# A hybrid decoder layer in fp32 on one core: the memory norm moved behind the key matmuls, combinations of x on VectorE, and a memory region set apart for the first operands of three stages

## The chip, the cores and the metric

The kernel runs on one core of one Trainium2 chip (trn2). The metric is the device time of one execution in microseconds (us), lower is better. Engines are named as the profile names them: PE is TensorE (matmuls; PEld is its weight load), DVE is VectorE, ACT is ScalarE, POOL is GpSimd, SP is SyncE, which here only issues DMAs. Each engine runs its own instruction stream in order.

## What is computed

One decoder layer on x (1024 tokens by 1024 channels) with 256 memory tokens, cut to what matters here:

```
h = rms_norm(x, g_mix);  z = h @ w_in                       # 13,312 columns
ret  = swish(rg) * head_norm(retention(rq, rk, rv), g_ret)   # 4 heads, chunks of 128
da   = head_norm(diff_attention(dq, dk, dv, lam), g_diff)    # 4 heads, causal, ALiBi
kv   = rms_norm(mem, g_mem) @ w_mem_kv;  mk, mv = halves of kv
ca   = softmax(cq @ mk.T / 16) @ mv                          # 4 heads
x   += (g0*(ret @ w_ret_o) + g1*(da @ w_diff_o) + g2*(ca @ w_cross_o)) @ w_out
u    = relu(rms_norm(x, g_ffn) @ w_up);  x += (u*u) @ w_down  # 4096 wide
out  = rms_norm(x, g_final)
```

`rms_norm(m, g)` scales each token by r = 1/sqrt(mean(m*m) + 1e-6) and each channel by g. As r is one number for each token, it can be applied to the rows of a product as well as to its operand.

## The kernel before

All activations are held with channels on the partitions and tokens along the free dimension, in tiles of 128 x 512 (`t` is the half of the tokens). An fp32 operand is split into a high and a low part (`split`, lines 143 to 145: a CAST on ACT writes the high part, a subtraction on DVE the low part), and a product is three matmuls, high by high, high by low, low by high (`mm3`, lines 153 to 159). These three lines, L157 to L159, are where nearly all matmuls are recorded.

The two widest products, z (52 units of 256 columns) and the MLP's up projection (16 units), use a scheme of seven block products in place of eight (`seven`, line 243). For each unit `left_operands` (line 210) loads two blocks of weights (tile `wr`), forms their combinations (`ws`) and splits seven operands into tiles `wo`, of which 11 exist; `quad` multiplies one of them with one of seven combinations of the input (`hop`). These combinations (B11, B21, T1 to T4, B22) are made once, ahead of the stage.

The stages follow each other in this order, with the lines of their code:

- **Start** (lines 283 to 413). `mt`, the memory tokens, are summed in squares (`wide_sums`), `rms_finish` makes the row factors, and `scale_rows` makes the normed tokens `mh`. Then come 8 key blocks (`mem_keys`) and 4 heads of values (`mem_values`); their results leave PSUM through `kv_store` (L377, a copy on ACT into one of three `kvs` tiles) and go to DRAM (`mk_d`, `mv_d`). Between them the generator `x_steps` norms x and makes the combinations of x; two of them for each `kp` are subtractions on POOL (L361, L362).
- **z** (lines 416 to 484). Results go to DRAM (`zh_d` holds q of the cross attention already split).
- **Cross attention** (from line 573). `cross_inputs` loads and splits mk and mv of a head, `cross_probs` loads q (`cq`) and computes the scores `csc`, and `cross_values` transposes the probabilities (`ctp`).
- **Differential attention**, with matmuls of the cross branch's output projection as filler.
- **Retention** (lines 809 to 965), 32 steps of a chunk each. `rec_load` (L828) loads a chunk's record (1280 KB) on ACT's DMA queue into one of three `rec` tiles, `ret_prepare` computes the scores `rsc`, `ret_product` the states `rst`. The filler is the rest of the branch projections (`y`).
- **Output projection and second norm** (lines 969 to 1024). Row sums of squares are added on POOL (`acc`, L1006); the new residual goes to DRAM (`xs_d`).
- **Up** (lines 1027 to 1048). The last two combinations of the normed x (`df`, L1044) are subtractions on POOL; `u_emit` stores u to DRAM.
- **Down** (lines 1051 to 1117). `down_chunk` loads u (into `ur`) and w_down (into `dwr`) and splits them into `u` and `dw`; chunks hold 2, 2, 4, 4, ... blocks of 128 rows of w_down (`CHUNKS`). The accumulators `x2` (tiles `xm`) are loaded with the residual first (L1106, 16 DMAs of 256 KB), and each chunk's product is added to them (L162, `xm<-xm,dn`). The final norm works on two halves of the last columns.

Pools on the "right" side are opened and closed stage by stage, so a tile of the next stage can be filled only when the memory of the stage before it has been released. A scheduler fixes the order of the instructions on each engine and DMA queue when the kernel is built; the DMAs of SP's queue are issued in that order, and one that waits holds back those behind it.

## Time and profile before

| | us |
|---|---|
| median of 3 runs | 2685.02 |
| lowest and highest | 2679.22, 2689.7 |
| the profiled execution, its own time | 2690.2 |
| its span in the profile | 2688.2 |
| PE busy in it | 2565.5 |
| mean granted clock of PE | 0.983 |

The span runs from the first to the last instruction. A row of the timeline gives the start of a piece of work, its length, and in square brackets how long its engine stood idle ahead of it and what ended that wait. "Busy" of PE is the time in which at least one matmul was under way, at either clock; matmuls overlap, so the mean duration of one is longer than the distance between two. The profiled execution took 5.2 us more than the median.

### The profile page before, as it was taken

What the parts mean: (1) busy time and instruction counts of PE and PEld (TensorE: products, weight loads), DVE (VectorE), ACT (ScalarE), POOL (GpSimd) and SP (SyncE); (2) the same over time, 40 slices, a digit from 0 to 9 for tenths busy, and PEclk for the clock granted to TensorE, in tenths of its full rate; (3) what the DMA queues carried; (4) which work ended last, traced back from release to release, by engine and by line L of the source; (5) the groups of instructions that cost most, each with busy time, mean ns of one, the idle gap of its engine ahead of it and who ended that gap; (6) DMA issues with size and microseconds to landing.
All of it is one profiled execution on the core that took longest, in us unless ns stands there. A gap on an engine that the chain in (4) does not pass through costs nothing. (4 is left out here: it accounts for less than half of the span.)

```text
span 2688.2 us, 32542 instructions
## 1 busy us (share of the span) xinstructions
PE 2565.5 (95%) x11878; PEld 2100.5 (78%) x11878; DVE 1588.2 (59%) x2831; ACT 1055.4 (39%) x1942; POOL 119.4 (4%) x125
## 2 busy tenths in 40 slices
PE   7899999999999999899996999999979999899998
PEld 6688887788888888688885787878868888688887
DVE  6666656665566544276774666663676565654435
ACT  4444444444344444355553223231544444311212
POOL 3000000000000000000110000000230000000001
PEclk9999999999999999999998999999989999999999
DMA  5444457755543333264448776753523332632311
GB/s 208 155 167 162 166 154 204 212 163 154 145 118 114 109 111 100 100 263 165 171 157 308 252 239 240 255 175 95 176 98 115 112 107 79 240 114 85 110 40 63
DMA packets 250416, 416.63 MB, mean 155 GB/s; under 512 B 16912, under 2 KB 147984, under 8 KB 242064
## 3 DMA queue, kind: packets, MB, share of 16 engines
q1 hardware_dynamic: 231680, 351.60, 40.3%
q10 hardware_dynamic: 18576, 62.96, 6.6%
q8 instruction: 93, 1.52, 0.2%
q14 instruction: 67, 0.55, 0.1%
HBM read 273.98 MB, written 140.51 MB: 154 GB/s over the span
## 5 line engine op out<-in xcount | busy, mean ns | idle before, releaser
L157 PE MATMUL x<-hop,wo 128*128 128x512 f32 x1904 | 751.7, 395 | 15.6 <-ACT wo L144 13.9
L158 PE MATMUL x<-hop,wo 128*128 128x512 f32 x1904 | 751.2, 395 | 0.0
L159 PE MATMUL x<-hop,wo 128*128 128x512 f32 x1904 | 745.2, 391 | 0.3 <-DVE wo L145 0.3
L157 PEld LDWEIGHTS x<-hop,wo 128*128 128x128 f32 x1904 | 359.1, 189 | 93.8 <-ACT wo L144 14.3
L159 PEld LDWEIGHTS x<-hop,wo 128*128 128x128 f32 x1904 | 358.6, 188 | 81.7 <-DVE wo L145 2.1
L158 PEld LDWEIGHTS x<-hop,wo 128*128 128x128 f32 x1904 | 359.1, 189 | 74.3
L144 ACT CAST wo<-wr 128x512 fp32r<-128x512 f32 x272 | 168.1, 621 | 242.0 <-PE x L159 233.6
L145 DVE TENSOR_TENSOR wo<-ws,wo 128x512 fp32r<-128x512 f32 x204 | 140.8, 692 | 197.4 <-ACT wo L144 197.3
L145 DVE TENSOR_TENSOR wo<-wr,wo 128x512 fp32r<-128x512 f32 x272 | 186.3, 687 | 92.1 <-ACT wo L144 92.0
L157 PE MATMUL dn<-u,dw 128*128 128x512 f32 (+1 forms) x544 | 206.7, 380 | 10.0 <-DVE xm L162 5.3
L158 PE MATMUL dn<-u,dw 128*128 128x512 f32 (+1 forms) x544 | 206.3, 379 | 0.0
L159 PE MATMUL dn<-u,dw 128*128 128x512 f32 (+1 forms) x544 | 206.0, 379 | 0.0
L162 DVE TENSOR_TENSOR zo<-x,s 128x512 f32<-128x512 f32 x156 | 107.6, 690 | 157.3 <-ACT s L272 109.7
L162 DVE TENSOR_TENSOR xm<-xm,dn 128x512 f32<-128x512 f32 (+1 forms) x152 | 99.0, 657 | 145.0 <-PE dn L159 138.7
L144 ACT CAST wo<-ws 128x512 fp32r<-128x512 f32 x204 | 126.3, 621 | 91.0 <-PE x L159 85.2
L157 PEld LDWEIGHTS dn<-u,dw 128*128 128x128 f32 x544 | 103.1, 189 | 31.0 <-DVE xm L162 6.8
L162 DVE TENSOR_TENSOR g<-y,g 128x512 f32<-128x512 f32 x64 | 44.2, 690 | 129.9 <-PE y L159 96.0
L159 PEld LDWEIGHTS dn<-u,dw 128*128 128x128 f32 x544 | 103.0, 189 | 19.9 <-DVE dw L145 0.8
L158 PEld LDWEIGHTS dn<-u,dw 128*128 128x128 f32 x544 | 103.1, 189 | 19.1 <-issue 0.2
L157 PE MATMUL y<-ar,whl 128*128 128x512 f32 x256 | 102.2, 400 | 9.1 <-ACT ar L144 9.1
L158 PE MATMUL y<-ar,whl 128*128 128x512 f32 x256 | 101.4, 396 | 1.4 <-DVE ar L145 1.4
L159 PE MATMUL y<-ar,whl 128*128 128x512 f32 x256 | 100.6, 393 | 0.0
(235 smaller groups left out, 4057.6 us busy)
## 6 DMA issues: line engine op xcount, KB each, us to landing
wr<-in_w_z SPq DMA_DIRECT2D x104, 512.0 KB, 4.0
rec<-rc ACTq DMA_DIRECT2D x32, 1280.0 KB, 7.8
zh<-zh SPq DMA_DIRECT2D x48, 512.0 KB, 3.4
rc<-zth SPq DMA_DIRECT2D x96, 256.0 KB, 3.6
rc<-zh SPq DMA_DIRECT2D x64, 256.0 KB, 3.7
g<-z SPq DMA_DIRECT2D x64, 256.0 KB, 4.1
wr<-in_w_up SPq DMA_DIRECT2D x32, 512.0 KB, 4.0
u<-uo ACTq DMA_DIRECT2D x64, 256.0 KB, 2.0
```

Source lines behind the costliest of these rows:

```text
L144: nc.scalar.copy(out=hl_hi, in_=src)
L145: eng.tensor_tensor(out=hl_lo, in0=src, in1=hl_hi.bitcast(F32), op=ALU.subtract)
L157: nc.tensor.matmul(out, ah, bh, start=first, stop=False, skip_group_check=again)
L158: nc.tensor.matmul(out, ah, bl, start=False, stop=False, skip_group_check=again)
L159: nc.tensor.matmul(out, al, bh, start=False, stop=last, skip_group_check=again)
L162: nc.vector.tensor_tensor(out=out, in0=a, in1=b, op=op)
```

## The change

It has six parts.

1. The memory tokens are only multiplied by `g_mem` ahead of the key and value matmuls. Their norm (`mem_norm`) is computed after the matmuls of the first key block, and is applied in `kv_store`: to keys by a DVE multiplication with a row (`mem_row`), to values by the scale of the ACT copy (`mem_r`).
2. The two POOL subtractions of each step of x, and the eight POOL subtractions `df` ahead of up, become DVE subtractions (`add`).
3. A pool `c0` of one tile (`ahead`) stays open from the end of the start stage to the end of the output projection. Before the z stage ends it takes the first q of the cross attention and the split keys of head 0; after the cross attention it takes the record of the first retention chunk. To make room, `wo` has 9 tiles in place of 11.
4. A pool `d0` holds the first block of w_down and of u, loaded and split while up runs; the first two chunks of down hold 1 and 3 blocks in place of 2 and 2.
5. u is loaded straight into the low half of its tile and split there, without the `ur` staging tile.
6. The first chunk's product is copied from PSUM into `x2` by ACT; the residual is loaded later (`xres`) and added by POOL after chunks 3 and 4.

```
-    *_, acc = wide_sums(mt)
-    add(acc[:, :NMEM], acc[:, :NMEM], acc[:, NMEM:HALF])
-    rb = rms_finish(acc, NMEM)
...
-        scale_rows(mem_of(k), src, vec[:, V_MEM + k : V_MEM + k + 1], rb[:, :NMEM])
+        nc.vector.tensor_scalar(
+            out=mem_of(k), in0=src, scalar1=vec[:, V_MEM + k : V_MEM + k + 1], scalar2=None, op0=ALU.mult
+        )
...
-            nc.gpsimd.tensor_tensor(out=b12, in0=b22, in1=b12, op=ALU.subtract)
-            nc.gpsimd.tensor_tensor(out=t4, in0=b21, in1=t2, op=ALU.subtract)
+            add(b12, b22, b12, ALU.subtract)
+            add(t4, b21, t2, ALU.subtract)
...
+    def mem_norm():
+        *_, acc = wide_sums(mt)
+        add(acc[:, :NMEM], acc[:, :NMEM], acc[:, NMEM:HALF])
+        nc.scalar.copy(out=mem_row, in_=rms_finish(acc, NMEM, mem_r)[:, :NMEM])
+
+    def kv_store(dst, o, r):
         st = sp0.tile([P, 256], F32, tag="kvs", name="kvs", bufs=3)
-        nc.scalar.copy(out=st, in_=o)
+        if r is None:
+            add(st, o, mem_row, ALU.mult)
+        else:
+            nc.scalar.activation(out=st, in_=o, func=AF.Copy, scale=r)
         nc.sync.dma_start(out=dst, in_=st)
...
+    c0p = cx.enter_context(tc.tile_pool(name="c0p", bufs=1, side="right", reuse_waits="tile"))
...
+    def z_between(i):
+        if i == NU - 3:
+            c = ahead_tile()
...
+            nc.sync.dma_start(out=q.bitcast(F32), in_=zh_d[CQ][0])
+            raw = zt.tile([P, HALF], F32, tag="zo", name="mkr", bufs=4)
+            nc.sync.dma_start(out=raw, in_=mk_d[0].rearrange("p d c -> p (d c)"))
...
-        q = load(qk_tile("q", "cq"), zh_d[CQ + h * 256][t])
+        q = ahead["q"] if h == t == 0 else load(qk_tile("q", "cq"), zh_d[CQ + h * 256][t])
...
+            if h == NH - 1 and i == 4:
+                ahead["rec"] = ahead_tile()
+                nc.sync.dma_start(out=ahead["rec"][:, :C_G].bitcast(F32), in_=rc_d[0][0][:, 0, :C_G])
...
-    for c in range(3):
+    recs.append(ahead["rec"])
+    for c in range(1, 4):
         rec_load(0, c)
...
-            if n + 2 < 8 * NH:
+            if 1 < n < 8 * NH - 2:
                 rec_load((n + 2) // 8, (n + 2) % 8)
...
+    CHUNKS = [range(0, 1), range(1, 4)] + [range(f, f + FC) for f in range(4, 32, FC)]
...
+                u = pool.tile([P, 2, HALF], F32R, tag="u", name="u", bufs=2 if c == 0 else 4 * FC)
+                nc.sync.dma_start(out=u[:, 1].bitcast(F32), in_=u_d[f][t])
+                split(u[:, 0], u[:, 1], u[:, 1].bitcast(F32))
...
+    def u_between(i):
+        if i == 13:
+            ahead["down"] = down_chunk(0, d0)
...
-            nc.gpsimd.tensor_tensor(out=df, in0=x3[kp][t][:, 1], in1=x3[kp][t][:, 0], op=ALU.subtract)
+            add(df, x3[kp][t][:, 1], x3[kp][t][:, 0], ALU.subtract)
...
-            add(x2[d][t][:, cols], x2[d][t][:, cols], o[:, :width])
+            if first:
+                nc.scalar.copy(out=x2[d][t], in_=o)
+            else:
+                add(x2[d][t][:, cols], x2[d][t][:, cols], o[:, :width])
...
+            if c in (3, 4):
+                for d in range(8):
+                    xr = zs_tile("sp", "xres", 3)
+                    nc.sync.dma_start(out=xr, in_=xs_d[d][c - 3])
+                    nc.gpsimd.tensor_tensor(out=x2[d][c - 3], in0=x2[d][c - 3], in1=xr, op=ALU.add)
```

`z_between` and `u_between` are called by `seven` after each unit; in `left_operands`, `bufs=11` becomes `bufs=9`.

How the change moves instructions is shown at three places. The first is SP's queue at the end of z, before the change: the last stores of z, a weight of the cross branch (`wst`), the keys and values of head 0 (`raw`) and the two halves of its q (`cq`).

```order
L427 DMA z_1_132<-zo 128x512 [waits DMAHW5_49,Activation_49]
L520 DMA g<-z_0_125 128x512 [waits DMAHW7_49,Pool_49]
L499 DMA wst<-in_w_co 128x1024 [waits DMAHW6_49]
L568 DMA raw<-mk_253 128x512 [waits DMAHW7_49]
L568 DMA raw<-mv_257 128x512 [waits DMAHW0_49]
L563 DMA cq<-zh_0_77 128x2048 [waits DMAHW1_49,PE_49]
L563 DMA cq<-zh_1_78 128x2048 [waits DMAHW2_49]
```

The same place of SP's queue after the change.

```order
L451 DMA z_1_132<-zo 128x512 [waits DMAHW6_49,Activation_49]
L556 DMA g<-z_0_125 128x512 [waits DMAHW7_49,Pool_49]
L535 DMA wst<-in_w_co 128x1024 [waits DMAHW0_49]
L604 DMA raw<-mv_257 128x512 [waits DMAHW1_49]
L599 DMA cq<-zh_1_78 128x2048 [waits DMAHW2_49]
L604 DMA raw<-mk_254 128x512 [waits DMAHW3_49]
```

The keys of head 0 and the first half of q stand earlier in the queue now, and the second half of q comes behind one load fewer of 256 KB and one fewer of 1 MB. On PE, 6 of the 24 first score matmuls now stand inside the last z unit and 18 right behind it.

The second place is PE at the change from differential attention to retention, before: `dot` are the last transposes of the attention, `y` the filler.

```order
L774 MATMUL dot<-ident,don 128x128 [waits Activation_49]
L774 MATMUL dot<-ident,don 128x128
L157 MATMUL rsc<-rec 128x128 [waits DMAHW5_49]
L158 MATMUL rsc<-rec 128x128
L159 MATMUL rsc<-rec 128x128
L157 MATMUL rsc<-rec 128x128
L158 MATMUL rsc<-rec 128x128
L159 MATMUL rsc<-rec 128x128
L157 MATMUL y<-ac_0_8861,whl 128x512 [waits DVE_49]
```

And after the change.

```order
L159 MATMUL y<-ac_1_8887,whl 128x512
L157 MATMUL rsc<-rec 128x128 [waits DMAHW6_49]
L158 MATMUL rsc<-rec 128x128
L159 MATMUL rsc<-rec 128x128
L157 MATMUL rsc<-rec 128x128
L158 MATMUL rsc<-rec 128x128
L159 MATMUL rsc<-rec 128x128
L157 MATMUL rst<-ahead 128x512
L158 MATMUL rst<-ahead 128x512
L159 MATMUL rst<-ahead 128x512
L157 MATMUL rst<-ahead 128x512 [waits DVE_49]
```

The scores of the first chunk (`rsc<-ahead`, 6 matmuls) have moved up among the attention's last matmuls. At the old place now stand the scores of the second chunk, which wait for that chunk's record, and six state matmuls of the first chunk ahead of `y`.

The third place is SP's queue where up ends and down begins, before.

```order
L1062 DMA ur<-u_0_173 128x512 [waits DMAHW1_49,DMAHW0_49,PE_49]
L1062 DMA ur<-u_1_174 128x512 [waits DMAHW5_49,DMAHW1_49]
L1067 DMA dwr<-in_w_down 128x1024 [waits DMAHW3_49,DVE_49,Pool_49]
L1062 DMA ur<-u_0_175 128x512 [waits DMAHW4_49]
L1062 DMA ur<-u_1_176 128x512 [waits DMAHW5_49]
L1067 DMA dwr<-in_w_down 128x1024 [waits DVE_49,DMAHW6_49,Activation_49,Pool_49]
L1106 DMA xm_0_19342<-xs_0_237 128x512 [waits DMAHW7_49]
L1106 DMA xm_1_19343<-xs_1_238 128x512 [waits DMAHW0_49,PE_49,Pool_49]
```

And after the change.

```order
L214 DMA wr<-in_w_up 128x1024 [waits DMAHW4_49]
L1162 DMA xres<-xs_0_237 128x512 [waits DMAHW5_49,DMAHW3_49,DMAHW6_49,DMAHW1_49,DMAHW7_49,DMAHW0_49,Activation_49]
L1080 DMA dwr<-in_w_down 128x1024 [waits DMAHW4_49,PE_49]
L1083 DMA u<-u_0_175 128x512 [waits DMAHW5_49]
L1083 DMA u<-u_1_176 128x512 [waits DMAHW7_49,DVE_49,Pool_49]
L1080 DMA dwr<-in_w_down 128x1024 [waits DMAHW0_49]
```

The first block's loads (`u_0_173`, `u_1_174` and its `dwr`) have moved up among the weight loads of up, the 16 `xm` loads are gone from here, and one `xres` load stands ahead of the second block's.

## Rows read from the trace of the kernel before

**Rows 1.** Page part 1: busy time of the engines over the span.

```profile
PE 2565.5 (95%) x11878; PEld 2100.5 (78%) x11878; DVE 1588.2 (59%) x2831; ACT 1055.4 (39%) x1942; POOL 119.4 (4%) x125
```

**Rows 2.** Timeline of PE, start stage (start, length, engine, line, work, idle before).

```profile
14.07 11.68 PE L384 MATMUL mk<-mh,kst 128*128 128x256 f32 x46 [0.57 <-DVE mh L200]
...
44.43 1.05 PE L170 MATMUL ssq<-ones,sqw 128*128 128x1 f32 x8 [1.50 <-DVE sqw L162]
...
93.26 0.79 PE L157 MATMUL x<-hop,wo 128*128 128x512 f32 x1 [6.34 <-ACT wo L144]
```

**Rows 3.** Timeline of PE, z to cross attention.

```profile
1143.32 0.55 PE L157 MATMUL csc<-mk,cq 128*128 128x256 f32 x1 [11.25 <-DMA cq<-zh]
...
1153.14 0.47 PE L157 MATMUL csc<-mk,cq 128*128 128x256 f32 x2 [0.81 <-DMA cq<-zh]
```

**Rows 4.** Timeline of PE, into retention.

```profile
1432.16 0.47 PE L157 MATMUL rsc<-rec 128*128 128x128 f32 x1 [6.28 <-DMA rec<-rc]
...
1436.97 0.79 PE L157 MATMUL y<-ac,whl 128*128 128x512 f32 x1 [3.27 <-DVE g L162]
```

**Rows 5.** Timelines of PE and POOL, start of up.

```profile
1981.81 0.79 PE L157 MATMUL x<-hop,wo 128*128 128x512 f32 x1 [7.53 <-ACT wo L144]
...
1994.52 2.05 PE L183 MATMUL rb<-dg,ones 128*128 128x512 f32 x2 [3.37 <-DVE dg L179]
...
1986.78 5.70 POOL L1044 TENSOR_TENSOR df<-x 128x512 f32<-128x512 f32 x3 [2.29 <-DVE hop L145]
```

**Rows 6.** Group of PE, 2306 to 2350 us, start of down (busy, mean ns; idle, releasers).

```profile
L157 PE MATMUL dn<-u,dw 128*128 128x512 f32 x44 | 18.7, 428 | 9.6 <-DVE xm L162 5.0 <-ACT dw L144 4.7
```

**Rows 7.** Groups of the start stage: PE, ACT, POOL (columns as before).

```profile
L394 PE MATMUL mv<-kst,mh 128*128 128x256 f32 x128 | 28.9, 383 | 7.1 <-ACT kvs L377 7.1
...
L144 ACT CAST hop<-xr 128x512 fp32r<-128x512 f32 x16 | 9.6, 618 | 9.9 <-POOL xr L203 4.8 <-POOL xr L361 3.6 <-DVE xr L200 1.5
L144 ACT CAST hop<-tt 128x512 fp32r<-128x512 f32 x12 | 7.3, 618 | 9.4 <-POOL tt L362 6.5 <-DVE hop L145 1.8 <-DVE tt L162 1.1
...
L361 POOL TENSOR_TENSOR xr<-xr 128x512 f32<-128x512 f32 x4 | 6.5, 1630 | 6.2 <-DVE tt L162 6.2
L362 POOL TENSOR_TENSOR tt<-xr,tt 128x512 f32<-128x512 f32 x4 | 6.5, 1630 | 3.3 <-DVE tt L162 1.9 <-ACT hop L144 1.4
```

**Rows 8.** Timeline of DVE, start stage.

```profile
57.19 0.68 DVE L145 TENSOR_TENSOR hop<-tt,hop 128x512 fp32r<-128x512 f32 x1
57.79 1.78 DVE L145 TENSOR_TENSOR hop<-xr,hop 128x512 fp32r<-128x512 f32 x1
```

**Rows 9.** DMA issues of 1135.9 and 1136.3 us (KB, us to landing).

```profile
cq<-zh SPq DMA_DIRECT2D x1, 1024.0 KB, 7.3
...
cq<-zh SPq DMA_DIRECT2D x1, 1024.0 KB, 9.4
```

**Rows 10.** Windows of PE: length, busy (matmuls), granted clock, DMA share, GB/s.

```profile
1143.30:1146.30 3.00, 2.98 (x14) 0.50 0.98 363
...
2311.00:2314.30 3.30, 3.24 (x7) 0.50 0.67 250
2314.50:2317.80 3.30, 3.30 (x16) 1.00 0.76 255
```

**Rows 11.** DMA issue of 1425.9 us: the second record.

```profile
rec<-rc ACTq DMA_DIRECT2D x1, 1280.0 KB, 10.2
```

**Rows 12.** Timeline of SP's queue, start of down.

```profile
2307.60 12.98 SPq L1106 DMA_DIRECT2D xm<-xs  x16
```

**Rows 13.** Groups of ACT by shape, whole span.

```profile
L144 ACT CAST wo<-wr 128x512 fp32r<-128x512 f32 x272 | 168.1, 621 | 242.0 <-PE x L159 233.6 <-DMA wr<-in_w_z 5.2 <-issue 3.1
...
L272 ACT COPY s<-x 128x512 f32<-128x512 f32 x68 | 39.9, 586 | 152.2 <-PE x L159 152.2
...
L144 ACT CAST dw<-dwr 128x1024 fp32r<-128x1024 f32 x32 | 33.0, 1051 | 165.9 <-PE dn L159 136.9 <-DMA dwr<-in_w_down 28.1 <-DVE xm L162 0.9
```

**Rows 14.** Window in down: length, then busy of PE, PEld, DVE, ACT, POOL; clock, DMA.

```profile
2420.00:2500.00 80.00, 80.00 (x355) 66.24 (x354) 36.56 (x52) 16.32 (x23) 0.00 (x0) 1.00 0.26 82
```

More of the change, by code (lines that the diff above doesn't have):

```diff
@@ L162, in add, with rms_finish @@
         nc.vector.tensor_tensor(out=out, in0=a, in1=b, op=op)
-    def rms_finish(acc, width):
+    def rms_finish(acc, width, keep=None):
         nt = width // P
@@ L174, in rms_finish @@
         )
-        r = tiny_tile(4, "rr")
+        r = tiny_tile(4, "rr") if keep is None else keep
         nc.gpsimd.tensor_tensor(out=r[:, :nt], in0=v[:, :nt], in1=mhalf[:, :nt], op=ALU.pow)
@@ L223, in left_operands @@
         ):
-            w = pool.tile([P, 2, HALF], F32R, tag="wo", name="wo", bufs=11)
+            w = pool.tile([P, 2, HALF], F32R, tag="wo", name="wo", bufs=9)
             split(w[:, 0], w[:, 1], src)
@@ L241, in quad, with seven @@
             )
-    def seven(units, ops, load, tmp, emit):
+    def seven(units, ops, load, tmp, emit, between=None):
         def begin(u):
@@ L413, in hybrid_block, with ahead_tile @@
     start.close()
+    cx = ExitStack()
+    c0p = cx.enter_context(tc.tile_pool(name="c0p", bufs=1, side="right", reuse_waits="tile"))
+    ahead = {}
+    def ahead_tile():
+        return c0p.tile([P, C_N], F32R, tag="c0", name="ahead")
     zw = ExitStack()
@@ L573, in cross_inputs @@
     def cross_inputs(h):
-        mk = load_halves(cp.tile([P, 2, 2, NMEM], F32R, tag="k", name="mk", bufs=2), mk_d[h])
+        mk = ahead["mk"] if h == 0 else load_halves(cp.tile([P, 2, 2, NMEM], F32R, tag="k", name="mk", bufs=2), mk_d[h])
         mv = load_halves(cp.tile([P, 2, 2, 256], F32R, tag="mv", name="mv", bufs=2), mv_d[h])
@@ L1024, in hybrid_block @@
     wpx.close()
+    cx.close()
+    d0 = ctx.enter_context(tc.tile_pool(name="d0", bufs=1, side="right", reuse_waits="tile"))
     ux = ExitStack()
@@ L1029, in hybrid_block, with down_chunk @@
     ut = ux.enter_context(tc.tile_pool(name="ut", bufs=2, side="right", reuse_waits="tile"))
+    FC = 4
+    CHUNKS = [range(0, 1), range(1, 4)] + [range(f, f + FC) for f in range(4, 32, FC)]
+    def down_chunk(c, pool):
+        ws, us = [], [[], []]
+        for f in CHUNKS[c]:
+            raw = pool.tile([P, 1024], F32, tag="wr", name="dwr", bufs=1 if c == 0 else 2)
+            nc.sync.dma_start(out=raw, in_=w_down[f])
+            for t in range(2):
+                u = pool.tile([P, 2, HALF], F32R, tag="u", name="u", bufs=2 if c == 0 else 4 * FC)
+                nc.sync.dma_start(out=u[:, 1].bitcast(F32), in_=u_d[f][t])
+                split(u[:, 0], u[:, 1], u[:, 1].bitcast(F32))
+                us[t].append(u)
+            w = pool.tile([P, 2, 1024], F32R, tag="w", name="dw", bufs=1 if c == 0 else FC + 2)
+            split(w[:, 0], w[:, 1], raw)
+            ws.append(w)
+        return ws, us
+    def u_between(i):
+        if i == 13:
+            ahead["down"] = down_chunk(0, d0)
     def u_emit(u, n, t, a, b):
@@ L1055, in hybrid_block, with mlp_down @@
     x2 = [[dw.tile([P, HALF], F32, name=f"xm{d}_{t}", tag=f"xm{d}_{t}", bufs=1) for t in range(2)] for d in range(8)]
-    def down_chunk(c):
-        ws, us = [], [[], []]
-        for f in CHUNKS[c]:
-            for t in range(2):
-                raw = dw.tile([P, HALF], F32, tag="ur", name="ur", bufs=4)
-                nc.sync.dma_start(out=raw, in_=u_d[f][t])
-                u = dw.tile([P, 2, HALF], F32R, tag="u", name="u", bufs=4 * FC)
-                split(u[:, 0], u[:, 1], raw)
-                us[t].append(u)
-            raw = dw.tile([P, 1024], F32, tag="wr", name="dwr", bufs=2)
-            nc.sync.dma_start(out=raw, in_=w_down[f])
-            w = dw.tile([P, 2, 1024], F32R, tag="w", name="dw", bufs=FC + 3)
-            split(w[:, 0], w[:, 1], raw)
-            ws.append(w)
-        return ws, us
-    def mlp_down(chunk, t, c0=0, width=HALF):
+    def mlp_down(chunk, t, c0=0, width=HALF, first=False):
         ws, us = chunk
@@ L1101, in final_norm @@
             nc.sync.dma_start(out=outT[k0 : k0 + n, :, c : c + width].rearrange("k p c -> p k c"), in_=y)
-    nxt = down_chunk(0)
-    for d in range(8):
-        for t in range(2):
-            nc.sync.dma_start(out=x2[d][t], in_=xs_d[d][t])
+    nxt = ahead["down"]
     for c in range(len(CHUNKS)):
@@ L1109, in hybrid_block @@
         if c + 1 < len(CHUNKS):
-            nxt = down_chunk(c + 1)
+            nxt = down_chunk(c + 1, dw)
             for t in range(2):
-                mlp_down(cur, t)
+                mlp_down(cur, t, first=c == 0)
+            if c in (3, 4):
[3 more added lines that the diff above has]
+                    nc.gpsimd.tensor_tensor(out=x2[d][c - 3], in0=x2[d][c - 3], in1=xr, op=ALU.add)
     mlp_down(cur, 0)
```

22 lines of the change are left out of this document (15 added, 7 removed).

## Prediction

> **What bounds the kernel now.** First the busy times of the page: PE works for 2565.5 of 2688.2 us, DVE for 59%, ACT for 39%, POOL for 4% [rows 1]. No part of the change takes a matmul away, so PE's busy time stays, and what can be won is PE's idle time (2688.2 - 2565.5 = 122.7 us) and what it costs that the granted clock is low after some of it. So the next view is the timeline of PE, read for rows with a long wait in brackets. The change aims at five of these places: the start (6.34 us ahead of the first z matmul [rows 2], and 7.1 us among the value matmuls [rows 7]), z to cross attention, 11.25 us [rows 3], into retention, 6.28 and 3.27 us [rows 4], the start of up, 7.53 and 3.37 us [rows 5], and the start of down, 9.6 us in all [rows 6]. They sum to 54.5 us; for each the reader should see what ends the wait: a DMA, ACT, or DVE. Last come the windows, which tell the clock: 14 matmuls in 3.0 us at a granted clock of 0.50, that is 1.2 of 2.4 GHz, and in down 7 matmuls in 3.3 us at 0.50 against 16 at 1.00 [rows 10].
>
> **Start.** The key matmuls begin at 14.07 after waiting for DVE [rows 2], and no longer need the norm of the memory, so the first block can begin some us earlier, when its weights are there. I give this lead no value: PE's next wait is for the squares of x from DVE, as at 44.43 [rows 2], and DVE's chain up to there is not shortened. It gets up to eight key multiplications, each at most the 0.68 us of a subtraction twice as wide [rows 8]; not all lie ahead of that point, and I charge 0.7 us. The gain is behind it. The value matmuls stand idle for 7.1 us, waiting for the copies `kvs` on ACT [rows 7]; in ACT's queue these stand behind casts that waited 3.6 and 6.5 us for the POOL subtractions L361 and L362 [rows 7]. These POOL operations take 1.63 us each [rows 7], and a DVE subtraction takes 1.78 us in place of 0.68 while POOL works [rows 8]. With eight of them moved, DVE saves 8 x 1.1 = 8.8 us and pays 8 x 0.68 = 5.4. So DVE gains 3.4 us and ACT's 10.1 us of waits shrink; I take 4.7 of PE's 7.1 us, less 0.7: **4 us**. Bounds: 0, if casts still arrive late from a DVE that has more to do, and 7.1. The 6.34 us ahead of z stay, because the first weights are issued behind the last `kvs` store in both.
>
> What DVE pays beside POOL can be weighed against a rule. The row shows a loss of 1.1 us for one DVE operation beside a POOL operation of 1.63 us [rows 7, 8]. The Trainium skill (SBUF — State Buffer, "Who interferes with whom") says that a DVE instruction with two SBUF inputs and a GpSimd one that reads SBUF lock each other out, the later one waiting for the whole of the earlier. By that rule a DVE operation could lose up to 1.63 us, the moved ones would free 8 x 1.63 - 5.4 = 7.6 us of DVE in place of 3.4, and the start would give about 7 us. I keep the row.
>
> **z to cross attention.** z ends at 1143.32 - 11.25 = 1132.07, and PE waits for the first half of q [rows 3], which lands at 1135.9 + 7.3 = 1143.2; the second lands at 1136.3 + 9.4 = 1145.7 [rows 9]. With the first half and the keys of head 0 loaded during z, 24 matmuls run at once and PE waits for the second half. This now stands where the first stood, with 256 KB fewer ahead (0.7 us at 363 GB/s [rows 10]): about 1142.5. Before, the second group began after 24 matmuls, 16 of them at half clock: 1143.3 + 4.9 = 1148.2. That is 5.7 us, to which come 8 transposes already done (0.9), while the second group now meets the half clock (-1.6): **5 us**. Bounds: 0, if the queue holds the second half as late as it held both; 8, if also the 0.81 us at 1153.14 [rows 3] goes and the transposes' wait for the softmax is free. The six score matmuls inside the last z unit cost nothing: they are moved, not added. The nine `wo` tiles are a rival below.
>
> **Into retention.** The first record is loaded during the attention, but the matmuls at the old place now need the second record. That is issued first on ACT's queue, so it lands where the first did, 1432.1, instead of 1425.9 + 10.2 = 1436.1 [rows 4, 11]. So the 6.28 us stay (and the six moved matmuls leave it a little longer). Six state matmuls now run ahead of `y`, and every load behind has 1280 KB less ahead of it, some 3.5 us; they can fill most of the 3.27 us [rows 4] and more later, and I take **2.5 us**. Bounds: +6 if the later records' lead carries on, -3 if the load during the attention delays its own loads.
>
> **Start of up.** Three POOL subtractions hold POOL for 5.70 us, and the second norm's factor is queued behind them; its wait on PE is 3.37 us [rows 5]. Both go, but the eight subtractions (8 x 0.68 = 5.4 us) stand in DVE's queue ahead of the low part of the second `wo`, for which PE waits after its first matmuls. What is gained at the second norm is waited for there: **0.5 us**, bounds -1.5 and 3.
>
> **Start of down.** Here 9.6 us are idle, 4.7 for ACT's cast of the first weights and 5.0 for DVE, which waits for the residual [rows 6], 16 loads that hold SP's queue for 12.98 us [rows 12]. Two stretches of 3.3 us at half clock lose about half of each, 3.4 us in all (one shown [rows 10]). So 13 us could go. In their place comes a new wait: ACT must copy 16 results of the first chunk (0.586 us each, 9.4 us), and cast three weights (3 x 1.05) and six u (6 x 0.62) [rows 13], 16.2 us in order, while the first chunk's 48 matmuls take 11. Some 5 us of it ends late, and one stretch of half clock may stay (1): **7 us**. Bounds: 3, where the second block's weights come late too, as one `xres` load that waits for the last u stores stands ahead of them; 12. The 16 POOL additions later cost PE nothing: at up to 1.1 us of DVE each they take 18 us in two chunks of some 44 us, and DVE is busy for 36.56 of 80 us there [rows 14].
>
> **The sum.** 4 + 5 + 2.5 + 0.5 + 7 = 19 us. The profiled execution took 2690.2 us, so 2671.2 on its terms; it lies 5.2 above the median of 2685.0, so **2666 us** for the median.
>
> **Rivals.** *The gains are taken back by what is late next* (same). ACT bounds the first two chunks of down, which then give 3, and in the start DVE's longer chain leaves 0; with 5 + 2.5 + 0.5 that is 11 us: 2674. For it: ACT's 16.2 us against 11. Against it: PE has the second chunk, 33 us long, in which ACT can catch up. Chance 0.2. *It does not do what it says at the two record places* (same): PE waits as long for the second half of q and the second record as it did for the first, so that only 4 + 0.5 + 7 = 11.5 us come: 2673.5. For it: the 6.28 us that I leave in place; against it: the order of the queues. Chance 0.13. *Nine tiles are too few* (slower). `wo` serves 68 units in z and up. ACT's casts into it already wait 233.6 us for PE to release a tile [rows 13], so the number of tiles does bind ACT. A tile less means that each cast comes one quad of 12 matmuls later, about 2.85 us ((1132.07 - 93.26) / 52 units / 7 quads). With nine, a released tile is needed again eight quads on, 22 us, against 0.62 + 0.69 us for the split; only if other work delays ACT by over 20 us would PE wait. If each unit waited 0.5 us, it would be 34 us: 2666 + 34 = 2700. Chance 0.04.
>
> **The numbers.** Forecast 0.6; rivals 0.2, 0.13 and 0.04; 0.03 is for what I have not seen. A change of 0.5%, 13.4 us, is about what a measurement of this kernel can tell. Faster by that means under 2671.6: **0.6**. Within it: 0.2 + 0.13 + 0.02 = **0.35**. Slower: 0.04 + 0.01 = **0.05**. All upper bounds together would give 36 us (2649), all lower ones -1.5 (2687); as neither end is likely for five places at once, I take **2652 to 2682**, which takes in the two rivals on the same side and leaves out the slower one.
>
> **What would show it.** In the new profile: the value matmuls with under 3 us of waits; the second score group starting near 1142.5 less what the start gave; a wait of about 6 us still ahead of the second record; the first `dn` matmul right behind the last of up, then a wait for ACT's copies in the second chunk of about 5 us; no new waits for `wo` in z or up. It would be wrong if PE's rows in z show waits for casts, if the wait for q keeps its 11 us, or if down's first 45 us again hold 9 us of waits.

## The result and the profile after

The changed kernel took 2651.7 us (median of 4 runs, 2648.4 to 2654.6) against 2685.8 before: a ratio of 0.9875 with a 95% interval of [0.9851, 0.9899], some 34 us. A second series of 6 runs gave 2655.6 us and 0.9885 [0.9864, 0.9905], some 31 us. The forecast was 2666, from 2652 to 2682: the sign and the places were right, and the gain was 1.6 to 1.8 times the 19 us forecast. The first series lies 0.3 us past the lower end of the range, the second 3.6 us inside it.

The page of the changed kernel, busy times over the span, which answers to [rows 1]:

```profile
span 2647.6 us, 32432 instructions
...
PE 2559.5 (97%) x11878; PEld 2099.2 (79%) x11878; DVE 1568.7 (59%) x2839; ACT 1064.2 (40%) x1951; POOL 115.1 (4%) x125
```

The profiled executions differ by 2688.2 - 2647.6 = 40.6 us. PE's idle time fell from 122.7 to 88.1 us (34.6), and its busy time by 6.0, as the mean granted clock rose from 0.983 to 0.986; no matmul was taken away. The timeline of PE at the places of [rows 2 to 5]: the start, cross attention, retention, up (start, length, work, idle ahead and what ended it).

```profile
7.48 6.51 PE L397 MATMUL mk<-mh,kst 128*128 128x256 f32 x16 [7.48 <-DMA kst<-in_w_kv]
...
84.38 0.79 PE L157 MATMUL x<-hop,wo 128*128 128x512 f32 x1 [5.57 <-ACT wo L144]
...
1129.75 1.17 PE L658 MATMUL ctp<-ident,cp 128*128 128x128 f32 x4 [6.25 <-DVE cp L650]
1132.29 1.12 PE L658 MATMUL ctp<-ident,cp 128*128 128x128 f32 x4 [1.38 <-DVE cp L650]
1133.25 0.55 PE L157 MATMUL csc<-ahead,cq 128*128 128x256 f32 x1
...
1416.15 0.47 PE L157 MATMUL rsc<-rec 128*128 128x128 f32 x1 [5.61 <-DMA rec<-rc]
...
1449.24 0.50 PE L158 MATMUL y<-ad,whl 128*128 128x512 f32 x1 [2.12 <-DVE ad L145]
...
1470.45 0.62 PE L157 MATMUL y<-ad,whl 128*128 128x512 f32 x1 [2.03 <-ACT ad L144]
...
1946.76 0.80 PE L157 MATMUL x<-hop,wo 128*128 128x512 f32 x1 [4.23 <-ACT wo L144]
...
1955.30 2.04 PE L183 MATMUL rb<-dg,ones 128*128 128x512 f32 x2 [1.24 <-DVE dg L179]
1963.13 0.80 PE L159 MATMUL x<-hop,wo 128*128 128x512 f32 x1 [5.79 <-DVE wo L145]
```

And the groups of the value matmuls and of the start of down, which answer to [rows 6, 7]:

```profile
L409 PE MATMUL mv<-kst,mh 128*128 128x256 f32 x128 | 27.8, 379 | 0.0
...
L157 PE MATMUL dn<-u,dw 128*128 128x512 f32 x46 | 18.5, 402 | 5.8 <-ACT xm L1134 3.9 <-DVE xm L162 1.6 <-DVE uo L162 0.3
```

The reader should see that the 7.1 us among the value matmuls are gone altogether, that the 11.25 us ahead of the first scores have become 6.25 and 1.38 ahead of the transposes of their softmax, that the second record is waited for 5.6 us as forecast, and that at up and in down waits of another kind (DVE's `wo`, ACT's `xm`) stand where the old ones stood.

Where the time came from is read best at the same instruction of PE in both traces. Besides the rows already shown these are, first before the change and then after it:

```profile
1413.52 0.50 PE L157 MATMUL y<-ac,whl 128*128 128x512 f32 x1 [1.50 <-DVE g L162]
...
1494.40 0.50 PE L157 MATMUL y<-ad,whl 128*128 128x512 f32 x1 [3.10 <-ACT ad L144]
...
1802.59 0.50 PE L157 MATMUL y<-ar,whl 128*128 128x512 f32 x1 [1.45 <-ACT ar L144]
...
1996.83 0.80 PE L159 MATMUL x<-hop,wo 128*128 128x512 f32 x1 [0.27 <-DVE wo L145]
```

```profile
1397.81 0.50 PE L157 MATMUL y<-ac,whl 128*128 128x512 f32 x1 [1.50 <-DVE g L162]
...
1772.30 0.50 PE L157 MATMUL y<-ar,whl 128*128 128x512 f32 x1 [1.44 <-ACT ar L144]
```

The table gives the time from one such instruction to the next. The next to last column is the same gain between the second profiles of the two kernels, which are told of below.

| Stretch of PE, up to | before | changed | gain | second profiles | forecast |
|---|---|---|---|---|---|
| the first z matmul | 93.3 | 84.4 | 8.9 | 10.9 | 4 |
| the last filler in the differential attention | 1320.3 | 1313.4 | 6.9 | 1.6 | 5 |
| the last wait for `ad` in early retention | 80.9 | 72.6 | 8.3 | 6.6 | 2.5 |
| the last wait for `ar` in retention | 308.2 | 301.8 | 6.4 | 12.5 | 0 |
| the fifth matmul of up | 194.2 | 190.8 | 3.4 | 3.8 | 0.5 |
| the end | 691.4 | 684.5 | 6.9 | 9.2 | 7 |

The fifth matmul of up is the first of L159, the third product of its group, and the expectations below call it the third; PE runs two matmuls of the next group ahead of it. It runs at half clock in both kernels (granted clock 0.50). At the 85th matmul of up, with the granted clock at 1.00 in both, the gain of that row is 2.2 us (214.2 to 212.0) and that of the last row 8.1. Between the two rows of retention some work has moved: five `rst` and three `ro` matmuls that stand behind the wait for `ad` before the change stand ahead of it afterwards, which at 0.229 us each (an estimate) is 1.8 us of the 6.4.

### The profile page after: what moved, and what is told of

Its sections match the earlier page's. It is cut to its first block, busy times and chain, and to the rows that moved or that the text cites. A ratio compares the mean times of both kernels' runs of the same rounds, so it can differ in the third digit from the quotient of the medians.

```text
span 2647.6 us, 32432 instructions
## 1 busy us (share of the span) xinstructions
PE 2559.5 (97%) x11878; PEld 2099.2 (79%) x11878; DVE 1568.7 (59%) x2839; ACT 1064.2 (40%) x1951; POOL 115.1 (4%) x125
## 3 DMA queue, kind: packets, MB, share of 16 engines
q1 hardware_dynamic: 231824, 352.91, 40.6%
## 5 line engine op out<-in xcount | busy, mean ns | idle before, releaser
L159 PE MATMUL x<-hop,wo 128*128 128x512 f32 x1904 | 748.2, 393 | 5.8 <-DVE wo L145 5.8
L159 PEld LDWEIGHTS x<-hop,wo 128*128 128x128 f32 x1904 | 358.8, 188 | 88.3 <-DVE wo L145 7.6
L159 PE MATMUL dn<-u,dw 128*128 128x512 f32 (+1 forms) x544 | 205.1, 377 | 0.0
L162 DVE TENSOR_TENSOR xm<-xm,dn 128x512 f32<-128x512 f32 (+1 forms) x136 | 88.5, 654 | 133.7 <-PE dn L159 133.1
L159 PEld LDWEIGHTS dn<-u,dw 128*128 128x128 f32 x544 | 102.4, 188 | 19.0 <-issue 0.2
L157 PE MATMUL y<-ar,whl 128*128 128x512 f32 x256 | 102.2, 400 | 4.8 <-ACT ar L144 4.8
L158 PE MATMUL y<-ar,whl 128*128 128x512 f32 x256 | 101.3, 396 | 2.5 <-DVE ar L145 2.5
L144 ACT CAST whl<-wst 128x1024 fp32r<-128x1024 f32 x48 | 50.4, 1050 | 126.5 <-PE y L159 87.9
```

The source lines that it names most:

```text
L144: nc.scalar.copy(out=hl_hi, in_=src)
L157: nc.tensor.matmul(out, ah, bh, start=first, stop=False, skip_group_check=again)
L158: nc.tensor.matmul(out, ah, bl, start=False, stop=False, skip_group_check=again)
L159: nc.tensor.matmul(out, al, bh, start=False, stop=last, skip_group_check=again)
L162: nc.vector.tensor_tensor(out=out, in0=a, in1=b, op=op)
```

## The experiments

Each kernel undoes or adds one thing, but for down_as_before, which undoes parts 4 to 6 together, and three_together. Ratios are to the kernel before, which ran beside each of them.

| Kernel | median us | ratio, 95% interval |
|---|---|---|
| changed, second series | 2655.6 | 0.9885 [0.9864, 0.9905] |
| no_early_record | 2663.4 | 0.9909 [0.9895, 0.9922] |
| no_early_q | 2660.7 | 0.9901 [0.9887, 0.9914] |
| norm_first | 2652.8 | 0.9881 [0.9866, 0.9897] |
| pool_combinations | 2659.4 | 0.9908 [0.9892, 0.9925] |
| down_as_before | 2657.6 | 0.9899 [0.9881, 0.9916] |
| df_on_pool | 2651.7 | 0.9880 [0.9866, 0.9895] |
| up_weights_first | 2645.7 | 0.9844 [0.9826, 0.9862] |
| states_before_record | 2651.5 | 0.9876 [0.9859, 0.9894] |
| z_weights_early | 2648.0 | 0.9867 [0.9845, 0.9890] |
| three_together | 2633.0 | 0.9806 [0.9789, 0.9822] |

An interval spans 7 to 12 us, as much as a part is worth or more, so the verdict on a part rests on its waits and on the table's stretches, and the times only have to agree.

**Second profiles of both kernels.** Without an edit.

> The kernel before, unchanged, in a second profiled execution. Theory 1 (the waits that the change removed belong to the program): the waits at the five places come back within 1 us each (6.3 us ahead of z, 11.3 at the cross attention, 6.3 and 3.3 into retention, 7.5 at up, 9.6 at down), and also the waits for ar between 1635 and 1660 us (5.7) and at 1803 and 1806 us (2.9). Theory 2 (the 5.5 us that were won in the middle of retention, where the change moves nothing, are chance of one execution): the waits for ar differ by 2 us or more from these, while the five places stay.

> The changed kernel, unchanged, in a second profiled execution and timed. Theory 1: ratio 0.987 to 0.989 (2651 to 2656 us); between the second record and the first up matmul PE needs 530.6 us as in the first profile (1416.2 to 1946.8), within 1 us. Theory 2: that stretch differs by 2 us or more from 530.6.

The kernel before again: 6.40 us ahead of z, 11.57 at the cross attention, 7.18 and 2.55 into retention, 7.53 at up, 8.8 at the start of down; the waits for `ar` were 7.1 and 2.1. All came back within 1 us but for `ar`, 1.4 more and 0.8 less. But the changed kernel needed 527.4 us from the second record to up in place of 530.6 (1420.9 to 1948.3), beyond the 1 us of theory 1. So the waits at the five places belong to the program. The stretch in the middle of retention does not repeat well: 308.2 and 310.0 us before; 301.8 and 297.5 for the changed kernel; and 299.5 to 307.4 in the ten kernels below, most of which leave that stage's code as it is. So neither theory holds whole: a spread of several us comes without any edit to that stage, yet both profiles of the kernel before lie above all twelve others. That z to the attention gains only 1.6 us in the second profiles is due to a stretch in which PE ran slower (last section): it costs the changed kernel some 3.7 of its 1318.1 us, and the kernel before at least as much in its last row.

**Without the early record.**

```
-            if h == NH - 1 and i == 4:
-                ahead["rec"] = ahead_tile()
...
-    recs.append(ahead["rec"])
-    for c in range(1, 4):
+    for c in range(3):
         rec_load(0, c)
...
-            if 1 < n < 8 * NH - 2:
+            if n + 2 < 8 * NH:
```

> The changed kernel without the early load of the first retention record: all records are loaded as before. Theory 1 (the record's 1280 KB less at the boundary let all loads behind it land earlier): the y wait of 3.3 us and the waits for ad of 11.7 us in all come back, retention loses about 8 us against the changed kernel: some 2659 us. Rival (the gain there comes from the order that the scheduler chose on ACT and DVE, or from chance, not from the record): under 3 us lost, 2652 to 2655 us. If the 5.5 us in the middle of retention also hang on the record, 13 us are lost: 2665 us.

Early retention took 81.6 us against 72.6 and 73.3, as long as before (80.9). The times agree: 0.9909 against 0.9885, 6.4 us. The timeline of PE of this kernel, into retention and then at the waits for `ad`:

```profile
1416.06 0.48 PE L157 MATMUL rsc<-rec 128*128 128x128 f32 x1 [6.43 <-DMA rec<-rc]
...
1419.21 0.80 PE L157 MATMUL y<-ac,whl 128*128 128x512 f32 x1 [1.61 <-DVE g L162]
...
1451.11 0.80 PE L157 MATMUL y<-ad,whl 128*128 128x512 f32 x1 [4.00 <-ACT ad L144]
...
1457.62 0.79 PE L158 MATMUL y<-ad,whl 128*128 128x512 f32 x1 [4.13 <-DVE ad L145]
...
1473.23 0.50 PE L158 MATMUL y<-ad,whl 128*128 128x512 f32 x1 [1.06 <-DVE ad L145]
...
1478.85 0.79 PE L157 MATMUL y<-ad,whl 128*128 128x512 f32 x1 [4.19 <-ACT ad L144]
```

13.4 us of waits for `ad` stand here against 5.1 in the changed kernel (its five rows between 1446 and 1471 add up to 6.1, with those under 0.6 us), the wait for the record is longer by 0.8, and half of the `y` wait of 3.3 us is back. So the early record is worth 8 to 9 us by this stretch, and little of it at its own place. Taken together with the middle of retention it is more: from the last filler of the attention to the last wait for `ar`, the eleven profiles with the early record need 370.8 to 381.3 us (the changed kernel 374.5 and 370.8), this kernel 386.7, and the kernel before 389.1 and 389.9. So 12.2 of the two rows' 14.6 us go with the record, by one profile of this kernel.

The reason that theory 1 gives, that loads land earlier with 1280 KB less ahead of them, is not what the traces show. `ad` is cast from `pr`, 512 KB that SP loads some 30 us behind the records. SP's queue at that point, for the changed kernel and then for this one:

```profile
1437.98 0.38 SPq L855 DMA_DIRECT2D pr<-da  x1
1441.42 1.69 SPq L561 DMA_DIRECT2D mg<-g  x2
```

```profile
1440.93 0.32 SPq L561 DMA_DIRECT2D mg<-g  x1
...
1446.94 0.86 SPq L852 DMA_DIRECT2D pr<-da  x2
```

With the early record the scheduler puts the first `pr` ahead of a store (`mg`) that waits for a result; without it `pr` stands behind this store and a reload of it. It is issued 27 to 31 us after the first record loaded behind the attention in the eleven profiles with the early record, and 38 or 39 us in the three without; it lands 5.9 us later in the changed kernel and 3.5 us later here, so it is no quicker. The waits for `ad` shrink because of the order in SP's queue. The edit changes that order together with the traffic, and no run separates the two.

**Without the early q.**

```
-        q = ahead["q"] if h == t == 0 else load(qk_tile("q", "cq"), zh_d[CQ + h * 256][t])
+        q = load(qk_tile("q", "cq"), zh_d[CQ + h * 256][t])
```

with the same for the keys, and no loads in `z_between`.

> The changed kernel without the early q and keys of the cross attention. Theory 1 (the second half of q takes the first half's place in the queue): the wait of 11 us ahead of the first scores comes back, and 7 to 9 us are lost: 2659 to 2661 us. Rival (PE waits in any case for the softmax and for q's second half, so the early q is worth little): under 4 us lost, 2652 to 2656 us.

The timeline of PE of this kernel at the first scores of cross attention:

```profile
1136.16 0.55 PE L157 MATMUL csc<-mk,cq 128*128 128x256 f32 x1 [12.48 <-DMA cq<-zh]
...
1145.96 0.47 PE L157 MATMUL csc<-mk,cq 128*128 128x256 f32 x2 [0.79 <-DMA cq<-zh]
```

It shows the wait of before, 12.5 us, and the 0.8 us at the third load of q. From z to the end of the differential attention it took 1321.4 us, 8 more than the changed kernel. The profiles with the early q took 1311.3 to 1314.6, but for two with a slow stretch of PE (1318.1 and 1318.3), those of the kernel before 1320.3 and 1319.6. By the times it is 4 us (0.9901 against 0.9885), within the intervals. Theory 1 holds.

**The two halves of the start.** In the first kernel the memory norm stands ahead of the keys again, in the second the combinations of x are back on POOL.

```
-            add(b12, b22, b12, ALU.subtract)
-            add(t4, b21, t2, ALU.subtract)
+            nc.gpsimd.tensor_tensor(out=b12, in0=b22, in1=b12, op=ALU.subtract)
+            nc.gpsimd.tensor_tensor(out=t4, in0=b21, in1=t2, op=ALU.subtract)
```

> The changed kernel with the memory norm back ahead of the key matmuls and the kvs copies back on ACT without a factor; the combinations of x stay on DVE. Theory 1 (the lead of 6.6 us at the first key block is used up by DVE before the value matmuls, and the start's gain comes from the POOL subtractions): the first z matmul starts within 1 us of the changed kernel's 84.4 us, the value matmuls still wait under 1 us, 2653 to 2656 us. Rival (half or more of the start's 8.9 us comes from the norm's new place): first z matmul at 88 us or later, 2657 us or more.

> The changed kernel with the two subtractions of each step of x back on POOL; the memory norm stays behind the first key block. Theory 1: the waits of the value matmuls for kvs come back (5 to 7 us), DVE's subtractions take up to 1.8 us beside POOL again, the first z matmul starts at 91 to 93 us: 2660 to 2663 us. Rival (the norm's new place brings the gain): first z matmul at 87 us or earlier, 2657 us or less.

The first z matmul and the value matmuls, for norm_first and then for pool_combinations:

```profile
13.76 12.70 PE L387 MATMUL mk<-mh,kst 128*128 128x256 f32 x46 [0.58 <-DVE mh L200]
...
85.39 0.80 PE L157 MATMUL x<-hop,wo 128*128 128x512 f32 x1 [5.38 <-ACT wo L144]
...
L397 PE MATMUL mv<-kst,mh 128*128 128x256 f32 x128 | 27.9, 380 | 0.0
```

```profile
L409 PE MATMUL mv<-kst,mh 128*128 128x256 f32 x128 | 29.1, 383 | 6.2 <-ACT kvs L390 6.2
...
92.61 0.79 PE L157 MATMUL x<-hop,wo 128*128 128x512 f32 x1 [6.36 <-ACT wo L144]
```

With the norm first, z starts 1.0 us later, although the keys start 6.3 us later; with POOL it starts 8.2 us later, and the 6.2 us of waits for `kvs` are back. So nearly the whole gain of the start comes from taking work off POOL. The part that the change's title names first is worth a microsecond at most: in eight profiles whose start is the same code as in the changed kernel, z begins between 84.1 and 85.4 us, and 85.39 lies among them. The times agree (0.9881 and 0.9908 against 0.9885).

**The down stage as before.** The code of before for up and down, with `df` on DVE.

```
-    CHUNKS = [range(0, 1), range(1, 4)] + ...
+    CHUNKS = [range(0, 2), range(2, 4)] + ...
```

> The changed kernel with the up and down stages' loads, chunks, staging and residual as before (df stays on DVE, wo has 9 tiles). Theory 1: the 9.6 us of waits at the start of down and two stretches of half clock come back, 7 to 8 us lost: 2660 to 2663 us. Rival (ACT's copies and the residual on POOL take back most of it): under 4 us lost, 2657 us or less.

The first group of down on PE in this kernel (2276 to 2322 us):

```profile
L157 PE MATMUL dn<-u,dw 128*128 128x512 f32 x44 | 18.9, 434 | 8.8 <-ACT dw L144 4.7 <-DVE xm L162 4.2
```

The waits are back: 8.8 us against 5.8. From the 85th matmul of up to the third chunk of down PE takes 346.7 us, as before the change (347.3), against 339.2 and 342.2 in the two profiles of the changed kernel: 7.5 or 4.5 us. The two differ because a stretch at half clock behind a wait for ACT's copy (2.97 us) comes in one and not in the other. The times give 4 to 6 us (0.9899 against 0.9885 and 0.9875). Theory 1 and its rival (under 4 us) are not parted by the times; the waits and the first profile speak for theory 1. Which of parts 4 to 6 does it isn't tested.

**df back on POOL.**

```
-            add(df, x3[kp][t][:, 1], x3[kp][t][:, 0], ALU.subtract)
+            nc.gpsimd.tensor_tensor(out=df, in0=x3[kp][t][:, 1], in1=x3[kp][t][:, 0], op=ALU.subtract)
```

> The changed kernel with the eight df subtractions ahead of up back on POOL. Theory 1 (what is gained at the second norm is waited for at the third matmul of the first unit, where DVE is late): the waits of 3.4 us for the norm's factor come back and the 5.8 us at the third matmul go, within 2 us of the changed kernel: 2653 to 2657 us. Rival (the subtractions on DVE are worth the whole of the norm's wait): 3 us or more lost, 2659 us or more.

The timeline of PE of this kernel at the start of up:

```profile
1949.29 0.80 PE L157 MATMUL x<-hop,wo 128*128 128x512 f32 x1 [7.52 <-ACT wo L144]
1953.57 2.08 PE L183 MATMUL rb<-dg,ones 128*128 128x512 f32 x2 [3.49 <-DVE dg L179]
...
1962.01 2.05 PE L183 MATMUL rb<-dg,ones 128*128 128x512 f32 x2 [3.37 <-DVE dg L179]
1964.32 0.80 PE L159 MATMUL x<-hop,wo 128*128 128x512 f32 x1 [0.27 <-DVE wo L145]
```

The way from the last wait for `ar` to the fifth matmul of up took 192.8 us against 190.8 and 191.1, with quite other waits ahead of its end: 7.5 us at the first matmul and 3.5 and 3.4 at the two norms, 0.3 at the fifth matmul. Behind it the clock rises sooner here, and to the 85th matmul it is 212.5 against 212.0 and 212.2. The times agree (0.9880 against 0.9885). Theory 1 holds: the edit moves waits and is worth half a microsecond.

**What still stands.** Three edits on the changed kernel follow from these readings. The first loads and splits the weights of the first up unit ahead of `df`:

```
+    first = left_operands(wu, w_up[0, 0], w_up[0, 1])
     for key, t in ((T3, 1), (T4, 0)):
...
-    seven(list(range(16)), hop2, lambda u: left_operands(wu, w_up[u, 0], w_up[u, 1]), ...)
+    seven(list(range(16)), hop2, lambda u: first if u == 0 else left_operands(wu, w_up[u, 0], w_up[u, 1]), ...)
```

> The changed kernel with the weights of the first up unit loaded, combined and split ahead of the df subtractions in the program. Theory 1 (at the start of up PE waits for DVE because the df subtractions stand ahead of the low part of wo): the wait of 5.8 us at the third matmul goes, 4 to 7 us won: 2646 to 2650 us. Rival (PE meets the missing df operands or the second norm instead, a wait as long in the first unit): within 2 us of the changed kernel.

The timeline of PE of this kernel at the start of up:

```profile
1953.59 0.80 PE L157 MATMUL x<-hop,wo 128*128 128x512 f32 x1 [4.23 <-ACT wo L144]
1955.83 2.08 PE L183 MATMUL rb<-dg,ones 128*128 128x512 f32 x2 [1.45 <-DVE dg L179]
```

These are the only waits over 0.6 us left there. The way from the last `ar` wait to the fifth matmul of up took 182.9 us against 190.8 and 191.1, and to the 85th 203.5 against 212.0 and 212.2: 8.5 us, more than expected. Two waits are gone, 5.79 and 1.24 us; the rest goes with the clock, which comes back sooner. The windows of PE behind the wait of the changed kernel, and then for this one (length, busy and matmuls, granted clock, DMA share, GB/s):

```profile
1963.00:1968.00 5.00, 4.87 (x12) 0.50 0.29 83
```

```profile
1964.00:1970.00 6.00, 6.00 (x27) 1.00 0.54 175
```

In the changed kernel PE idles for 5.79 us and then has 12 matmuls in 5 us at 0.50; with the weights first it works through and has 27 in 6 us at 1.00, though its up began 6.8 us later (1953.59 against 1946.76). Theory 1 holds, and the time, 2645.7 us, is just under its range.

The second takes the six state matmuls ahead of the wait for the second record:

```
+            if n == 1:
+                out = ret_product(h, c, cur, state)
             if n < 8 * NH:
                 prep = ret_prepare(n // 8, n % 8)
-            out = ret_product(h, c, cur, state)
+            if n > 1:
+                out = ret_product(h, c, cur, state)
```

> The changed kernel with the product of the first retention chunk (its rst matmuls) ahead of the scores of the second, which wait for the second record. Theory 1 (the wait of 5.6 us ends with the record's landing, whatever PE does before): the six matmuls move out of the half clock behind the wait, the wait shrinks by some 1.4 us and 1 to 3 us are won: 2649 to 2653 us. Rival (the waits for ad some 30 us later are set by DMA and take the gain back): no gain within 1 us, ad waits longer by as much.

The timeline of PE of this kernel into retention:

```profile
1415.81 0.30 PE L157 MATMUL rsc<-rec 128*128 128x128 f32 x1 [4.38 <-DMA rec<-rc]
...
1419.65 0.45 PE L157 MATMUL rsc<-rec 128*128 128x128 f32 x1 [2.74 <-DMA rec<-rc]
...
1426.42 0.73 PE L157 MATMUL y<-ac,whl 128*128 128x512 f32 x1 [2.86 <-DVE g L162]
```

The wait shrank by 1.2 us, and waits of 2.7 us for the third record and 2.9 for `g` took its place. Early retention took 72.3 us as in the changed kernel (72.6), and together with the middle of retention 373.6 against 374.5 and 370.8. There is no gain, as the rival says, but not for its reason: the waits for `ad` did not grow (4.7 us in all against 6.1).

The third opens the `c0` tile ahead of the start stage and loads the first z weights into it:

```
...
+    first_wr = ahead_tile()[:, :2048].bitcast(F32).rearrange("p (b a c) -> p b a c", b=2, a=2)
+    for j in range(2):
+        nc.sync.dma_start(out=first_wr[:, j], in_=w_z[0, j])
     for h in range(NH):
         mem_values(h)
...
```

> The changed kernel with the c0 tile opened ahead of the start stage and used for the weights of the first z unit, loaded beside the value matmuls. Theory 1 (the wait of 5.6 us ahead of z is the weights' load, issued behind the last kvs store): it falls to 1 or 2 us, and the z stage starts 4 to 5 us earlier: 2647 to 2651 us. Rival (the wo tiles lie in memory that the start stage releases late, or ACT's queue holds the cast): the wait stays above 4 us, no gain.

The timeline of PE of this kernel at the first z matmuls:

```profile
78.99 0.50 PE L157 MATMUL x<-hop,wo 128*128 128x512 f32 x1 [1.07 <-ACT wo L144]
...
80.90 0.50 PE L157 MATMUL x<-hop,wo 128*128 128x512 f32 x1 [1.17 <-ACT wo L144]
```

Two waits of 1.1 and 1.2 us are left of 5.6, and z starts 5.4 us earlier. Theory 1 holds.

> The three edits together on the changed kernel. Theory 1 (the places are independent, as the leads of the parts added up): the three gains add, 9 to 14 us: 2638 to 2645 us, ratio to the kernel before 0.982 to 0.985. Rival (a gain early in the program is given back at a wait that DMA sets later): under 7 us, 2646 us or more.

Together the three edits took 2633.0 us, ratio 0.9806 [0.9789, 0.9822]: faster than the changed kernel by 19 us going by the medians of the first series, and by 14.6 in the spans of the profiled executions (2633.0 against 2647.6).

The trace gives 5.2 us up to z and 9.5 at up, and nothing in retention. So the gains add, as theory 1 says, with the middle edit worth nothing, and the time is below the range expected. The rest of the 19 us is a choice of executions: the profiled one of the changed kernel was 2.0 us below its median (2649.7), that of this kernel 1.8 above (2634.8).

## Why the prediction was right, and where it was too small

- **Start, forecast 4, measured 8.9.** "I give this lead no value" and "I charge 0.7 us" held: the lead of 6.6 us (14.07 against 7.48) was used up, and at the squares of x the changed kernel is 0.55 us late (44.98 against 44.43). The step that failed is "I take 4.7 of PE's 7.1 us": all 7.1 went, the value matmuls themselves were busy for 1.1 us less (28.9 to 27.8), and another 0.8 went ahead of z (6.34 to 5.57). I took a part because DVE was to gain only 3.4 us, but the wait was one of ACT's queue, where a `kvs` copy stood behind casts that waited for POOL. ACT's casts of `hop<-tt` waited 9.4 us before, 6.5 of them for POOL [rows 7], and 4.5 after:

```profile
L144 ACT CAST hop<-tt 128x512 fp32r<-128x512 f32 x12 | 7.4, 619 | 4.5 <-DVE hop L145 3.6 <-DVE tt L162 0.9
```

  What DVE saves hardly matters where an in-order queue is held up by a third engine.
- **z to cross attention, forecast 5, measured 6.9.** The mechanism was right: the second half of q was issued at 1124.6 and landed 8.5 us later, and the second score group started at 1133.25. The forecast of "near 1142.5 less what the start gave" is 1133.6. That PE waits for nothing there is luck: the transposes, whose second four waited for the softmax until 1132.29, kept it busy until q landed, so an earlier q alone would have given next to nothing more. One term was off by 0.35: before, the second group began at 1147.85, not at 1148.2.
- **Into retention, forecast 2.5, measured 8.3.** The 5.6 us at the second record stayed, as said. Mis-sized is "they can fill most of the 3.27 us and more later": the "more later" was where the gain lay. The waits for `ad` fell from 11.7 to 5.1 us. The reason given, "1280 KB less ahead of it, some 3.5 us", isn't what brought it: the first load of `ad` went out 9 us sooner by its place in SP's queue and took no less time to land. The prediction priced the bytes and not the order of the queue, and left these waits to a bound.
- **The middle of retention, forecast 0, measured 6.4.** No term was there for it. The runs show 297.5 to 307.4 us for kernels that hold all or most of the change, and 308.2 and 310.0 without it; the spread is larger than the gain. Some 1.8 us are eight matmuls that moved ahead of the row, and taken with the row above, no_early_record gives back 12.2 of 14.6 us. So most of the two rows goes with the record, by one profile; by what path in the middle, beyond these matmuls, stays open.
- **Start of up, forecast 0.5, measured 3.4** at the fifth matmul and 2.2 at the 85th, with the clock up again in both. Of this 1.5 is a second wait for `ar` (at 1806.24 before) that was missing, so 0.7 is left for the place itself, and df_on_pool takes back 0.5. "What is gained at the second norm is waited for there" was right to the place: 5.79 us at the fifth matmul.
- **Start of down, forecast 7, measured 6.9**, or 8.1 from the 85th matmul of up. "Some 5 us of it ends late" was ACT's `xm`: 3.9 us in the group shown above. "One stretch of half clock may stay" came out either way: none in the first profile, one in the second (granted clock 0.71 from 2290 to 2296 us, behind the 2.97 us for `xm`), whose stretch from the 85th matmul on gains only 5.2 over the first profile of the kernel before. The POOL additions cost PE nothing (it is busy in all 88 us from 2372 to 2460), and here the trace agrees with the rule that the prediction drew on. A DVE subtraction of two SBUF operands went from 0.69 to 1.78 us at the most beside them, while the additions `xm<-xm,dn`, with one operand in PSUM, stayed at 0.69 (the second of the pair at 2378.03 runs into the POOL addition of 2378.84):

```profile
2378.03 1.27 DVE L162 TENSOR_TENSOR xm<-xm,dn 128x512 f32<-128x512 f32 x2
...
2378.84 2.54 POOL L1163 TENSOR_TENSOR xm<-xm,xres 128x512 f32<-128x512 f32 x2 [2.41 <-DVE xm L162]
```

  The Trainium skill (SBUF — State Buffer, "Who interferes with whom") says just this: a DVE instruction with at most one SBUF input, outside the 2-port perf modes, does not contend with GpSimd. For the size of the loss in the start, the row (1.1 us) and not the full lock (1.63) had been taken. The two are nearer than that: 14 of the 16 POOL additions took 1.29 us and two, which met a DVE subtraction as they began, 1.68, so the 1.63 of [rows 7] holds a wait of POOL's own. The error of that step came from ACT's queue and not from DVE, so that the lock's 7 us lie nearer to the 8.9 is no support for it.
- **The rivals.** Nine `wo` tiles cost nothing: all of PE's waits for ACT's `wo` in z and up, 9.8 us, are the first ones of the two stages (5.57 and 4.23); no run goes back to eleven. The gains were not taken back, and both record places did what they should, though the second gave its time elsewhere.
- **A sum.** The waits at the five places add up to 54.7 us, not 54.5; nothing hangs on it.

## What to carry to other kernels

Before valuing an edit by the engine whose work it cuts, look at what is queued behind the instruction that waits: here eight POOL operations of 1.6 us held ACT, ACT held the PSUM copies, and PE paid 8 us. Where a transfer is moved, compare the order of the other loads in the queues of the two programs, and not only the bytes ahead of them: here a load went out 9 us sooner because it came to stand ahead of a store that waits, and the time showed at waits some 40 to 60 us behind the records. Read a gain at a point where the clock is the same in both traces: 3.4 us at the start of up were 2.2 once it had risen. Where an edit moves a wait instead of removing it (`df`), look for the instruction that the waiting engine has in front of the needed one; putting that one first gave 8.5 us.

## What the runs showed of the hardware beyond that

In three of the fourteen traces PE ran some 2% slower for 200 to 300 us, with no wait and at a granted clock of 1.00. A window of the kernel before, in its first profile (columns as in [rows 14]; the counts in brackets are instructions):

```profile
2050.00:2250.00 200.00, 200.00 (x875) 164.12 (x874) 121.69 (x188) 85.36 (x147) 0.00 (x0) 1.00 0.32 107
```

The same window in its second profile:

```profile
2050.00:2250.00 200.00, 200.00 (x859) 162.01 (x858) 118.11 (x182) 81.91 (x141) 0.00 (x0) 1.00 0.33 109
```

Another window, of the changed kernel in its first profile:

```profile
110.00:290.00 180.00, 180.00 (x789) 147.67 (x787) 110.19 (x170) 80.90 (x140) 0.00 (x0) 1.00 0.49 173
```

And in its second profile:

```profile
110.00:290.00 180.00, 180.00 (x773) 146.10 (x772) 108.87 (x169) 79.72 (x138) 0.00 (x0) 1.00 0.48 169
```

859 matmuls stand against 875 in 200 us, and 773 against 789 in 180 us; DVE's and ACT's operations keep their durations. In the second profile of the kernel before these are 16 matmuls of 0.229 us, or 3.7 of its 2696.5 - 2688.2 = 8.3 us, in this window alone. The third trace is that of up_weights_first, with 773 matmuls from 110 to 290 us. The slow stretch is part of the spread from run to run, and what sets it off isn't shown by any of the runs.

A copy from PSUM on ACT took 0.1 us longer once it had a factor from a column of SBUF: the `kvs` copies of values (128 x 256) took 0.368 us on average before, and in the changed kernel:

```profile
L390 ACT ACTIVATE kvs<-mv,mem_r 128x256 f32<-128x256 f32 x8 | 3.8, 469 | 2.4 <-PE mv L409 2.4
```

The Trainium skill (ScalarE: Activation LUTs, "What ACT_TABLE_LOAD costs") gives about 93 ns for each such operand; the trace, with 0.101 us, agrees, though the instruction has also changed, from COPY to ACTIVATE, and no run separates the two.
